# Eight PSUM banks dealt anew between chunk preparation and RWKV chains

## The chip, the cores and the metric

The kernel runs on one core of one Trainium2 chip. The time is the device time of one execution in microseconds. Five engines work side by side, each through its own queue in order: TensorE (PE; its weight loads stand as PEld), VectorE (DVE), ScalarE (ACT), GpSimd (POOL) and SyncE (SP), which here issues most of the DMAs. PE writes its results to PSUM alone, which has eight banks of 512 float32 per partition; DVE and ACT empty them.

## The reference

One layer over 512 latent tokens and 256 context tokens of width 2048. RMSNorm with modulation from a condition vector (w_mod), one projection that feeds two groups of heads, an output projection, a gated feed-forward network with a 3x3 depthwise convolution, and a final RMSNorm. The mLSTM group has four heads in two directions. The RWKV group has 16 heads of width 64, also in two directions, and its state goes from token to token:

```
def step(s, xs):                       # state s: 64 x 64 per head
    r_t, w_t, k_t, v_t, kk_t, a_t = xs
    s = (s * w_t[:, :, None, :]
         - jnp.einsum("bhvk,bhk->bhv", s, kk_t)[..., None] * (kk_t * a_t)[:, :, None, :]
         + v_t[..., :, None] * k_t[..., None, :])
    return s, jnp.einsum("bhvk,bhk->bhv", s, r_t)
```

The context is scanned first from a zero state; each direction of the latent tokens starts from that direction's last context state.

## The kernel before, in words

**RWKV in chunks.** The scan is cut into chunks of 64 tokens: four for the context, eight for x. Heads go in pairs, one head on partitions 0 to 63 and one on 64 to 127; there are eight pairs. For each pair four things happen, one after the other.

- The preparation (`pair_shared`, `prep`). For x it is called once per direction; for the context both directions go through at once. It makes the decays and gates (matmuls L701, tanh L704), the running sum (L437), the operands KR and BK, and then in two halves of four chunks: products of BK and KR (L747) into two PSUM tiles, four masks (L750) into the SBUF tile r_Gp, a store of r_Gp to DRAM (L751). After that, again in two halves: a scaled copy of BK (L756, into r_cum), four transposes (L759) into one PSUM tile, four copies (L763) into r_sg, a store (L764). r_sg, r_cum, r_Gp, r_KR and r_BK have one buffer each, and r_sg is also what the tanh of the next preparation writes.
- The solve (`tsolve`): it inverts the triangular blocks, on DVE (L798, L799) and with small matmuls (L816, L821) behind a transpose (L810).
- The chain (`chain`, `chain_step`): eight steps for x, four for the context. In a step the state M and the values V are multiplied with the chunk's operands, ACT copies the sum to r_Rs (L872), matmuls give U, ACT copies that to r_U (L880), matmuls give the change of M, which DVE adds (L892), and for x the output y (L899 for the first half of the chunks, L901 after).
- The bonus and the finalization of y (`bonus`, `finalize_pair`).

Two pairs form a job for solve and chain.

**PSUM.** The eight banks are dealt to three tags: "acc" (the projections, two), "pre" (preparation, the early mLSTM heads, the w_mod sums, finalization, two) and "R" (solve and chain, four). A chain step of one pair takes two banks, one per head, with both directions in each; so the steps of two pairs, which alternate in the program, go through four banks.

**Order.** The program is unrolled. A planner lays down each engine's order ahead of time: it goes through the instructions by priority (the order in the program, with weight loads and their splits moved ahead) and through an assumed timeline, and puts the first one that is ready there next on its engine. So projections are put between the steps of preparation and chain. On the chip each engine then follows that order and waits where an operand or buffer is late. In the program, x goes pair by pair: `x_pair(p + 1)` with projections for the next pair, `x_job(p)` with solve or chain for earlier pairs and the preparation of pair p, then w_mod sums (`ada_late`: DVE sums L232, with one buffer am for the loads). After the last pair come its solve and chain, the mLSTM projections (`x_head`), three early mLSTM heads, which use SBUF tiles of the preparation, and the output projection, whose first half needs the mLSTM heads 0 and 1 and the RWKV pairs 0 to 3. In the step as it was, this is what the change turns round:

```
for src in range(2):           # 0: the state M, 1: the values V
    for k, u in enumerate(us): # the two directions of one pair
        for j in kinds:        # two products for x, one for the context
            for h in range(2): # the two heads, a bank each
```

Of the kernel before, what the change touches and what calls it, by code (L numbers as in the profile page):

```python
# [11 lines left out]
ALU = mybir.AluOpType  # L12
# [3 lines left out]
P = 128  # L16
# [80 lines left out]
def body(tc, A, dbg=None):  # L97
    nc = tc.nc
    pe, dve, act, pool, sp = nc.tensor, nc.vector, nc.scalar, nc.gpsimd, nc.sync
# [3 lines left out]
    def nm(s):  # L103
        cnt[0] += 1
        return f"{s}_{cnt[0]}"
# [17 lines left out]
    wp = Pool("wp")  # L123
    hp = Pool("hp")
    sm = Pool("sm")
    PB = {"acc": 2, "pre": 2, "R": 4}

    def PS(tag, shape):
        return ps.tile(list(shape), F32, tag=tag, name=nm(tag), bufs=PB[tag])

    def DT(tag, shape, bufs=1):
        return dr.tile(list(shape), F32, tag=tag, name=nm(tag), bufs=bufs)
# [11 lines left out]
    rk = Pool("rk")  # L144
# [192 lines left out]
    def wload(src, shape, slot=None):  # L337


        n = max(shape[1] // WPARTS, 1)  # L340
        his, los = [], []
        wn[0] += 1
        with tc.high_priority(ahead_[0]), tc.issue_after(last_wm[0].ins) if W_TIE < wn[0] <= 3 else nullcontext():
            raw = wp("wraw", shape, WRAW)
            if not isinstance(src, list):
                src = [src]
            m = shape[1] // len(src)
            for i, a in enumerate(src):
                last_w[0] = sp.dma_start(raw[:, i * m:i * m + m], a)
            for i in range(0, shape[1], n):  # L350
                sh = [P, n] + list(shape[2:])
                if slot is None:
                    hi = wp("whi", sh, WBUF, F32R)
                    lo = wp("wlo", sh, WBUF, F32R)
                else:
                    hi, lo = slot[:, 0, i:i + n], slot[:, 1, i:i + n]
                split(raw[:, i:i + n], hi, lo)
                his.append(hi)
                los.append(lo)
        return (lambda i: his[i // n][:, i % n]), (lambda i: los[i // n][:, i % n])  # L360
# [288 lines left out]
    LOHI = (slice(0, 64), slice(64, 128))  # L649
# [176 lines left out]
    def chain_load(u, tt):  # L826

        cu = u.c0 + 2 * tt
        o = rk("r_GK", [P, 2, 512], 6)[:, :, 0:3 * u.kc + 128]
        sp.dma_start(o, u.S_d[:, cu:cu + 2, :])  # L830
        return o

    def chain_v(p, seg, nch):

        t = rk("r_V", [P, 8, 64], 3)[:, 0:nch]
        for h, hs in enumerate(LOHI):
            o = (p % 2) * 128 + 64 * h
            sp.dma_start(t[hs], v_d[seg][p // 2, :, :, o:o + 64].rearrange("a (b t) v -> t (a b) v", t=64))
        return t

    def chain_step(us, ops, cs, V, y, first, last):

        x = us[0].seg == "x"
        kc = us[0].kc
        bank = [PS("R", [P, 8, 64]) for _ in range(2)]
        pos = (0, 1) if cs[0] < cs[1] else (1, 0)
        opened = {}

        def mm(h, half, o, w, rhs):

            hs = LOHI[h]
            out = bank[h][LOHI[half], o, :]
            at = opened.get((h, half))
            f = dict(stop=True, skip_group_check=True)
            if at is None:
                opened[(h, half)] = pe.matmul(out, w[hs], rhs[hs], start=True, **f)
                return
            with tc.issue_after(at.ins):
                pe.matmul(out, w[hs], rhs[hs], start=False, **f)  # L859

        w = [o[:, c % 2] for o, c in zip(ops, cs)]
        kinds = range(2) if x else range(1)
        for src in range(2):
            for k, u in enumerate(us):
                for j in kinds:
                    for h in range(2):
                        o = 2 * kc * src + 64 * j
                        mm(h, h if j == 0 else 1 - h, pos[k], w[k][:, o:o + 64], u.M if src == 0 else V[:, cs[k], :])
        Rs = rk("r_Rs", [P, 2, 64], 3)
        U = rk("r_U", [P, 2, 64], 3)  # L870
        for h, hs in enumerate(LOHI):
            act.copy(Rs[hs], bank[h][hs, 0:2, :])  # L872
        for k, u in enumerate(us):
            for h in range(2):
                mm(h, 1 - h, 2 + pos[k], w[k][:, kc:kc + 64], Rs[:, pos[k], :])
            for h in range(2):
                if not last:
                    mm(h, h, 2 + pos[k], w[k][:, 3 * kc + 64:3 * kc + 128], V[:, cs[k], :])
        for h, hs in enumerate(LOHI):
            act.copy(U[hs], bank[h][LOHI[1 - h], 2:4, :])  # L880
        for k, u in enumerate(us):
            for h in range(2):
                if not last:
                    mm(h, h, 2 + pos[k], w[k][:, 3 * kc:3 * kc + 64], U[:, pos[k], :])
            for h in range(2):
                if x:
                    mm(h, 1 - h, pos[k], w[k][:, kc + 64:kc + 128], U[:, pos[k], :])
        if not last:
            for k, u in enumerate(us):
                g = u.g0 + cs[k]  # L890
                for h, hs in enumerate(LOHI):
                    dve.scalar_tensor_tensor(u.M[hs], u.M[hs], u.gC[hs, g:g + 1], bank[h][hs, 2 + pos[k], :], ALU.mult, ALU.add)  # L892
        if x:
            lo, hi = min(cs), max(cs)
            for h in range(2):
                hs = LOHI[1 - h]
                out = y[hs, lo:hi + 1:hi - lo, :]
                if first:
                    dve.tensor_copy(out, bank[h][hs, 0:2, :])  # L899
                else:  # L900
                    dve.tensor_tensor(out, bank[h][hs, 0:2, :], out, ALU.add)  # L901

    def chain(pairs, mid):

        x = pairs[0][0].seg == "x"
        nch = pairs[0][0].nch
        Vs, ys = [], []
        for us in pairs:
            Vs.append(chain_v(us[0].p, us[0].seg, nch))
            ys.append(rk("r_yt", [P, 8, 64], 2) if x else None)  # L910
            for u in us:
                if not x:
                    Mst[(u.p, u.d)] = rk("r_M", [P, 64], 16)
                    pool.memset(Mst[(u.p, u.d)], 0.0)
                u.M = Mst[(u.p, u.d)]
        n = nch // 2
        for i in range(n):
            if x and i == 1:
                mid()
            ops = [[chain_load(u, i if u.d == 0 else n - 1 - i) for u in us] for us in pairs]  # L920
            for c in range(2 * i, 2 * i + 2):
                for us, o, V, y in zip(pairs, ops, Vs, ys):
                    chain_step(us, o, (c, nch - 1 - c), V, y, c < nch // 2, x and c == nch - 1)
        if x:
            for us, y in zip(pairs, ys):
                y_d = us[0].y_d = DT("yr_d", [4, P, 128], 8)
                for h in range(2):
                    sp.dma_start(y_d[:, :, 64 * h:64 * h + 64].rearrange("a (b t) v -> t (a b) v", t=64), y[LOHI[1 - h]])
            mid()
# [153 lines left out]
    for q, (k0, k1) in enumerate(KPARTS):  # L1083
        ks = slice(k0, k1)
        n = (k1 - k0) * P
# [47 lines left out]
    def do_chain(n=1):  # L1133
        if len(chain_q) >= n:
            job = [t for _ in range(n) for t in chain_q.pop(0)]
            chain([us for _, us, _ in job], fin_step)
            fin_q.extend(t for t in job if t[2] is not None)
# [215 lines left out]
    last, end = [], iter(())  # L1353
    for g in range(NG):
# [7 lines left out]
        for cs in (slice(0, NX),) if g < NG - 1 else (slice(0, NX // 2), slice(NX // 2, NX)):  # L1362
            n = cs.stop - cs.start
            su = ev() if g == NG - 1 else None
            for m2 in range(0, KT, 2):
                if g < NG - 1:
                    hi, lo = wload(A["wdn"][g, m2 // 2], [P, 2, GF, P])
                elif cs.start == 0:
                    last.append(wload(A["wdn"][g, m2 // 2], [P, 2, GF, P], hp("H", [P, 2, 2, GF, P], 8, F32R)))
                if g == NG - 1:  # L1370
                    hi, lo = last[m2 // 2]
# [129 lines left out]
```

## Time and profile before

| | |
|---|---|
| median of three runs | 3376.81 us (3371.88 to 3381.96) |
| the profiled execution | 3379.97 us |
| its span | 3378.2 us |
| mean granted PE clock | 0.945 of full speed |
| busy | PE 3108.0 us (92%), DVE 2165.9 (64%), ACT 1192.4 (35%), POOL 59.6 (2%) |
| DMA | 548.53 MB, 162 GB/s in the mean |

The profile is one execution. A busy PE is one with a matmul under way; it says nothing of how dense they are. The page's slices of 84 us show where PE has holes and where its granted clock falls: both lie between 1400 and 1700 us.

```
PE   8998899999989898657599899999999999999998
PEclk9999998899989898767799999999999999999999
```

In the rows below, times are microseconds from the start of the span, unless a column says ns.

### The profile page before, as it was taken

To read this page: it belongs to the slowest core of one execution; us is meant where nothing else is said; L and a number is where in the kernel's file an instruction comes from. 1 tells how busy PE (TensorE), PEld (TensorE's weight loads), DVE (VectorE), ACT (ScalarE), POOL (GpSimd) and SP (SyncE) were. 2 spreads that over 40 slices of the span, in tenths; PEclk is the share of its full clock that TensorE was granted. 3 is DMA by queue.
4 is the path that set the end of the run, shared out by engine and by line. 5 is a ranking of instruction groups with operands and counts; after the bars stand their busy time and mean duration, and the time that the engine had idled before them with its cause. 6 is when DMAs were issued, how large, how long until landed. Compare 5 with 4: busy or idle time off the path is not lost.

```text
span 3378.2 us, 54574 instructions
## 1 busy us (share of the span) xinstructions
PE 3108.0 (92%) x21030; PEld 2509.7 (74%) x21030; DVE 2165.9 (64%) x4178; ACT 1192.4 (35%) x2414; POOL 59.6 (2%) x113
## 2 busy tenths in 40 slices
PE   8998899999989898657599899999999999999998
PEld 5687777777768687545477688888888888888887
DVE  2587776688688778645644788455555555555657
ACT  4355554344444344222223432222222222322323
POOL 0000100010000000000000000000000000000000
PEclk9999998899989898767799999999999999999999
DMA  8877555557767687565844255222223222222232
GB/s 284 305 243 220 155 159 163 166 174 234 208 208 239 215 247 240 181 197 178 257 153 157 77 199 194 94 94 98 95 95 99 94 96 98 94 98 96 94 100 100
DMA packets 394387, 548.53 MB, mean 162 GB/s; under 512 B 151664, under 2 KB 272776, under 8 KB 393872
## 3 DMA queue, kind: packets, MB, share of 16 engines
q1 hardware_dynamic: 384480, 531.67, 49.3%
q10 hardware_dynamic: 9648, 13.37, 1.1%
q8 instruction: 166, 2.72, 0.3%
q14 instruction: 93, 0.76, 0.1%
HBM read 457.49 MB, written 87.47 MB: 161 GB/s over the span
## 4 chain that ended last, share of the span: by engine, by line
PE 53%; DMA 9%; DVE 6%; ACT 1%; issue 1%; SPq 1%; DVEq 0%; ACTq 0%
PE acc L371 10%; PE acc L372 10%; PE acc L370 10%; PE acc L1376 5%; PE acc L1378 5%; PE acc L1377 5%; DMA am<-in_wmod 3%; PE acc L1262 1%; PE pre L621 1%; PE acc L1263 1%; PE acc L1264 1%; DVE adacc L232 1%; DMA Sx_d<-r_sg 1%; PE R L859 1%; DMA x_d<-ev 1%
## 5 line engine op out<-in xcount | busy, mean ns | idle before, releaser
L299 ACT CAST whi<-wraw 128x512 fp32r<-128x512 f32 (+1 forms) x948 | 569.6, 604 | 1307.7 <-PE acc L371 678.6
L300 DVE TENSOR_TENSOR wlo<-wraw,whi 128x512 fp32r<-128x512 f32 (+1 forms) x948 | 628.4, 666 | 429.0 <-ACT whi L299 423.1
L370 PE MATMUL acc<-H,whi 128*128 128x512 f32 x1920 | 761.2, 396 | 6.1 <-ACT ev L520 4.0
L372 PE MATMUL acc<-H,wlo 128*128 128x512 f32 x1920 | 762.3, 397 | 1.2 <-DVE wlo L300 1.2
L371 PE MATMUL acc<-H,whi 128*128 128x512 f32 x1920 | 760.4, 396 | 0.0
L370 PEld LDWEIGHTS acc<-H,whi 128*128 128x128 f32 x1920 | 363.8, 189 | 87.5 <-ACT ev L520 4.3
L372 PEld LDWEIGHTS acc<-H,wlo 128*128 128x128 f32 x1920 | 364.2, 190 | 82.0 <-issue 4.9
L371 PEld LDWEIGHTS acc<-H,whi 128*128 128x128 f32 x1920 | 364.4, 190 | 78.8 <-issue 2.9
L1380 DVE SCALAR_TENSOR_TENSOR x<-acc,mod,x 128x512 f32<-128x512 f32 (+1 forms) x192 | 135.6, 706 | 221.7 <-PE acc L1378 221.6
L1324 DVE SCALAR_TENSOR_TENSOR f_cv<-upad,fvec,f_cv 128x512 f32<-128x512 f32 x352 | 263.8, 749 | 7.2
L1376 PE MATMUL acc<-fh,whi 128*128 128x512 f32 x640 | 253.2, 396 | 0.0
L1377 PE MATMUL acc<-fl,whi 128*128 128x512 f32 x640 | 253.1, 396 | 0.0
L1378 PE MATMUL acc<-fh,wlo 128*128 128x512 f32 x640 | 253.1, 396 | 0.0
L232 DVE SCALAR_TENSOR_TENSOR adacc<-am,csil,adacc 128x512 f32<-128x512 f32 x240 | 179.4, 748 | 83.7 <-DMA am<-in_wmod 81.6
L403 PE MATMUL acc<-whi,H 128*128 128x256 f32 x512 | 159.8, 313 | 2.2 <-ACT r_E L720 1.5
L405 PE MATMUL acc<-wlo,H 128*128 128x256 f32 x512 | 158.6, 311 | 1.6 <-DVE wlo L300 1.6
L404 PE MATMUL acc<-whi,H 128*128 128x256 f32 x512 | 156.0, 305 | 0.0
L1378 PEld LDWEIGHTS acc<-fh,wlo 128*128 128x128 f32 x640 | 120.2, 188 | 29.1
L1377 PEld LDWEIGHTS acc<-fl,whi 128*128 128x128 f32 x640 | 120.2, 188 | 29.0
L1376 PEld LDWEIGHTS acc<-fh,whi 128*128 128x128 f32 x640 | 120.2, 188 | 29.0
L1262 PE MATMUL acc<-H,whi 128*128 128x512 f32 x256 | 104.6, 414 | 32.4 <-DVE ev L1271 18.6
L750 DVE TENSOR_TENSOR r_Gp<-pre,c_gmask 64x512 f32<-64x512 f32 (+1 forms) x192 | 115.1, 599 | 18.1 <-DMA Sx_d<-r_Gp 11.6
(346 smaller groups left out, 4751.6 us busy)
## 6 DMA issues: line engine op xcount, KB each, us to landing
am<-in_wmod SPq DMA_DIRECT2D x128, 512.0 KB
wraw<-in_wup SPq DMA_DIRECT2D x88, 512.0 KB
wraw<-in_wgate SPq DMA_DIRECT2D x88, 512.0 KB
wraw<-in_wdn SPq DMA_DIRECT2D x88, 512.0 KB
wraw<-in_wcm SPq DMA_DIRECT2D x72, 512.0 KB
r_GK<-Sx_d SPq DMA_DIRECT2D x64, 512.0 KB
wraw<-in_wtm SPq DMA_DIRECT2D x56, 512.0 KB
Sx_d<-r_Gp SPq DMA_DIRECT2D x32, 512.0 KB
```

Of the source, the lines that this page charges most:

```text
L232: dve.scalar_tensor_tensor(acc, wm[:, k % 2], csil[:, k:k + 1], acc, ALU.mult, ALU.add)
L299: act.copy(hi, t)
L300: dve.tensor_tensor(lo, t, hi.bitcast(F32), ALU.subtract)
L370: pe.matmul(pt[:, :n], hi(k8), H.h(k), start=k == 0, stop=False)
L371: pe.matmul(pt[:, :n], hi(k8), H.l(k), start=False, stop=False)
L372: pe.matmul(pt[:, :n], lo(k8), H.h(k), start=False, stop=k == KT - 1)
L403: pe.matmul(o, H.h(k)[:, xs], hi(k4), start=first, stop=False, skip_group_check=True)
L405: pe.matmul(o, H.h(k)[:, xs], lo(k4), start=False, stop=k == KT - 1, skip_group_check=True)
L1324: dve.scalar_tensor_tensor(cv, u[:, a:a + GH, b:b + GW], fvec[:, f, tap:tap + 1], cv, ALU.mult, ALU.add)
L1376: pe.matmul(pt, hi(m)[:, k, :], th[:, cs], start=k == 0, stop=False)
L1377: pe.matmul(pt, hi(m)[:, k, :], tl[:, cs], start=False, stop=False)
L1378: pe.matmul(pt, lo(m)[:, k, :], th[:, cs], start=False, stop=k == GF - 1)
```

## The change

"pre" gets four banks and "R" two. A chain step now takes both pairs of a job and both directions, four units, in one pair of banks: one bank for each head, and in it four column blocks of 64 for the sums and four for the changes. So a copy to r_Rs or r_U moves 256 columns in place of 128, and there are half as many; r_Rs and r_U are one buffer of twice the width in place of three. Products with V are put before those with M. The updates of M and y keep their shapes and number.

```
-    PB = {"acc": 2, "pre": 2, "R": 4}
+    PB = {"acc": 2, "pre": 4, "R": 2}
...
-    def chain_step(us, ops, cs, V, y, first, last):
+    def chain_step(units, first, last):
...
-        for src in range(2):
-            for k, u in enumerate(us):
-                for j in kinds:
+        for src in (1, 0):
+            for u, w, c, V, n in units:
+                for j in range(2 if x else 1):
                     for h in range(2):
                         o = 2 * kc * src + 64 * j
-                        mm(h, h if j == 0 else 1 - h, pos[k], w[k][:, o:o + 64], u.M if src == 0 else V[:, cs[k], :])
-        Rs = rk("r_Rs", [P, 2, 64], 3)
-        U = rk("r_U", [P, 2, 64], 3)
+                        mm(h, h if j == 0 else 1 - h, n, w[:, o:o + 64], V[:, c, :] if src else u.M)
+        Rs = rk("r_Rs", [P, 4, 64], 1)
+        U = rk("r_U", [P, 4, 64], 1)
         for h, hs in enumerate(LOHI):
-            act.copy(Rs[hs], bank[h][hs, 0:2, :])
+            act.copy(Rs[hs], bank[h][hs, 0:4, :])
...
         for h, hs in enumerate(LOHI):
-            act.copy(U[hs], bank[h][LOHI[1 - h], 2:4, :])
+            act.copy(U[hs], bank[h][LOHI[1 - h], 4:8, :])
...
             for c in range(2 * i, 2 * i + 2):
-                for us, o, V, y in zip(pairs, ops, Vs, ys):
-                    chain_step(us, o, (c, nch - 1 - c), V, y, c < nch // 2, x and c == nch - 1)
+                units = []
+                for k, (us, os_, V, y) in enumerate(zip(pairs, ops, Vs, ys)):
+                    us[0].y = y
+                    for j, (u, o) in enumerate(zip(us, os_)):
+                        cu = nch - 1 - c if j else c
+                        units.append((u, o[:, cu % 2], cu, V, 2 * k + (j if 2 * c < nch - 1 else 1 - j)))
+                chain_step(units, c < nch // 2, x and c == nch - 1)
```

## Rows read from the trace of the kernel before

**Rows 1.** Busy time by stretch: engines, instructions, granted clock, DMA share, GB/s.

```profile
570.00:1366.00 796.00, 731.03 (x7976) 592.65 (x7974) 614.76 (x1371) 331.34 (x763) 25.18 (x40) 0.93 0.68 211
1395.00:1660.00 265.00, 152.27 (x1590) 111.88 (x1589) 145.50 (x355) 66.37 (x196) 1.72 (x8) 0.68 0.64 200
1960.00:3378.00 1418.00, 1401.67 (x6320) 1157.38 (x6319) 841.88 (x1292) 401.60 (x668) 0.00 (x0) 1.00 0.32 107
```

**Rows 2.** PE's waits, whole span: waiter, what ended it, sum, times, longest.

```profile
PE R L816 <- DVE t_X L810: 26.8, 6, 11.2
PE pre L238 <- DVE adacc L232: 22.9, 1, 22.9
PE acc L1262 <- DVE ev L1271: 18.6, 1, 18.6
...
PE R L859 <- ACT r_U L880: 12.1, 11, 1.7
...
PE R L859 <- ACT r_Rs L872: 9.3, 8, 3.0
...
PE R L856 <- DVE r_yt L899: 6.3, 10, 1.6
```

**Rows 3.** Timeline (start, duration, instruction): first and last of the x preparations.

```profile
570.21 1.12 PE L701 MATMUL pre<-r_lw,r_up 128*128 128x512 f32 x2
...
1364.76 1.50 ACT L763 COPY r_sg<-pre 64x256 f32<-64x256 f32 x4 [0.19 <-ACT r_Rs L872]
```

**Rows 4.** Timeline of DVE: the masks of two preparations.

```profile
1029.95 2.81 DVE L750 TENSOR_TENSOR r_Gp<-pre,c_gmask 64x512 f32<-64x512 f32 x4
...
1037.84 2.81 DVE L750 TENSOR_TENSOR r_Gp<-pre,c_gmask 64x512 f32<-64x512 f32 x4
...
1186.13 2.81 DVE L750 TENSOR_TENSOR r_Gp<-pre,c_gmask 64x512 f32<-64x512 f32 x4
...
1196.85 2.81 DVE L750 TENSOR_TENSOR r_Gp<-pre,c_gmask 64x512 f32<-64x512 f32 x4
```

**Rows 5.** Timeline of SP's queue: stores of the first of these preparations.

```profile
1032.79 0.37 SPq L751 DMA_DIRECT2D Sx_d<-r_Gp  x1
...
1043.16 0.58 SPq L764 DMA_DIRECT2D Sx_d<-r_sg  x1
...
1053.32 1.57 SPq L764 DMA_DIRECT2D Sx_d<-r_sg  x1
```

**Rows 6.** Timeline of PE: the same preparation.

```profile
1034.51 1.49 PE L747 MATMUL pre<-r_KR,r_BK 64*128 64x128 f32 x16
...
1040.78 0.60 PE L759 MATMUL pre<-c_ident,r_cum 128*128 128x128 f32 x4
```

**Rows 7.** Timeline of ACT: the same preparation and the next one's tanh.

```profile
1041.41 1.50 ACT L763 COPY r_sg<-pre 64x256 f32<-64x256 f32 x4 [0.68 <-PE pre L759]
...
1049.46 1.50 ACT L763 COPY r_sg<-pre 64x256 f32<-64x256 f32 x4 [6.55 <-PE acc L404]
...
1059.83 0.67 ACT L704 ACTIVATE r_sg<-pre,c_vecs 128x512 f32<-128x512 f32 x1
```

**Rows 8.** Groups by line: busy us, mean ns, idle before and its releasers.

```profile
L892 DVE SCALAR_TENSOR_TENSOR r_M<-r_M,r_gC,R 64x64 f32<-64x64 f32 x352 | 87.5, 278 | 28.5 <-PE R L859 21.9 <-ACT r_U L880 2.7
...
L880 ACT COPY r_U<-R 64x128 f32<-64x128 f32 x192 | 49.8, 260 | 80.7 <-PE R L859 75.1 <-DVE t_X L799 1.6 <-ACT ev L520 0.4
...
L899 DVE COPY r_yt<-R 64x128 f32<-64x128 f32 x64 | 18.5, 289 | 1.0
```

**Rows 9.** Timeline: the third x chain's last bank, the next solve.

```profile
1372.75 0.28 DVE L901 TENSOR_TENSOR r_yt<-R,r_yt 64x128 f32<-64x128 f32 x1
...
1447.87 1.92 PE L816 MATMUL R<-t_X,t_Y 32*32 32x32 f32 x64 [9.65 <-DVE t_X L810]
```

**Rows 10.** DVE's waits from 200 to 1960 us.

```profile
DVE adacc L232 <- DMA am<-in_wmod: 74.5, 44, 5.2
```

More of the change, by code (lines that the diff above doesn't have):

```diff
@@ L839, in chain_v @@
         return t
-    def chain_step(us, ops, cs, V, y, first, last):
-        x = us[0].seg == "x"
-        kc = us[0].kc
+    def chain_step(units, first, last):
+        x = units[0][0].seg == "x"
+        kc = units[0][0].kc
         bank = [PS("R", [P, 8, 64]) for _ in range(2)]
-        pos = (0, 1) if cs[0] < cs[1] else (1, 0)
         opened = {}
@@ L859, in mm @@
                 pe.matmul(out, w[hs], rhs[hs], start=False, **f)
-        w = [o[:, c % 2] for o, c in zip(ops, cs)]
-        kinds = range(2) if x else range(1)
-        for src in range(2):
-            for k, u in enumerate(us):
-                for j in kinds:
+        for src in (1, 0):
+            for u, w, c, V, n in units:
+                for j in range(2 if x else 1):
                     for h in range(2):
                         o = 2 * kc * src + 64 * j
-                        mm(h, h if j == 0 else 1 - h, pos[k], w[k][:, o:o + 64], u.M if src == 0 else V[:, cs[k], :])
@@ L869, in chain_step @@
-        Rs = rk("r_Rs", [P, 2, 64], 3)
-        U = rk("r_U", [P, 2, 64], 3)
+                        mm(h, h if j == 0 else 1 - h, n, w[:, o:o + 64], V[:, c, :] if src else u.M)
+        Rs = rk("r_Rs", [P, 4, 64], 1)
+        U = rk("r_U", [P, 4, 64], 1)
         for h, hs in enumerate(LOHI):
-            act.copy(Rs[hs], bank[h][hs, 0:2, :])
-        for k, u in enumerate(us):
+            act.copy(Rs[hs], bank[h][hs, 0:4, :])
+        for u, w, c, V, n in units:
             for h in range(2):
-                mm(h, 1 - h, 2 + pos[k], w[k][:, kc:kc + 64], Rs[:, pos[k], :])
+                mm(h, 1 - h, 4 + n, w[:, kc:kc + 64], Rs[:, n, :])
@@ L876, in chain_step @@
             for h in range(2):
                 if not last:
-                    mm(h, h, 2 + pos[k], w[k][:, 3 * kc + 64:3 * kc + 128], V[:, cs[k], :])
+                    mm(h, h, 4 + n, w[:, 3 * kc + 64:3 * kc + 128], V[:, c, :])
         for h, hs in enumerate(LOHI):
-            act.copy(U[hs], bank[h][LOHI[1 - h], 2:4, :])
-        for k, u in enumerate(us):
+            act.copy(U[hs], bank[h][LOHI[1 - h], 4:8, :])
+        for u, w, c, V, n in units:
             for h in range(2):
                 if not last:
-                    mm(h, h, 2 + pos[k], w[k][:, 3 * kc:3 * kc + 64], U[:, pos[k], :])
+                    mm(h, h, 4 + n, w[:, 3 * kc:3 * kc + 64], U[:, n, :])
@@ L885, in chain_step @@
             for h in range(2):
                 if x:
-                    mm(h, 1 - h, pos[k], w[k][:, kc + 64:kc + 128], U[:, pos[k], :])
+                    mm(h, 1 - h, n, w[:, kc + 64:kc + 128], U[:, n, :])
         if not last:
-            for k, u in enumerate(us):
-                g = u.g0 + cs[k]
+            for u, w, c, V, n in units:
+                g = u.g0 + c
                 for h, hs in enumerate(LOHI):
-                    dve.scalar_tensor_tensor(u.M[hs], u.M[hs], u.gC[hs, g:g + 1], bank[h][hs, 2 + pos[k], :], ALU.mult, ALU.add)
+                    dve.scalar_tensor_tensor(u.M[hs], u.M[hs], u.gC[hs, g:g + 1], bank[h][hs, 4 + n, :], ALU.mult, ALU.add)
@@ L893, in chain_step @@
         if x:
[L894 to L901, printed above, removed]
+            for k in range(0, len(units), 2):
+                cs = [units[k][2], units[k + 1][2]]
+                lo, hi = min(cs), max(cs)
+                y = units[k][0].y
+                for h in range(2):
+                    hs = LOHI[1 - h]
+                    out = y[hs, lo:hi + 1:hi - lo, :]
+                    if first:
+                        dve.tensor_copy(out, bank[h][hs, k:k + 2, :])
+                    else:
+                        dve.tensor_tensor(out, bank[h][hs, k:k + 2, :], out, ALU.add)
```

## The prediction

> **What bounds the kernel now.** I read the table of busy time by stretch first. From 1960 us on PE (TensorE) is busy 1401.67 of 1418 us at full clock, and the change touches nothing there [rows 1]. Two earlier stretches matter [rows 1]: from 570 to 1366 us PE is busy 731.03 of 796 us with DVE at 614.76, and from 1395 to 1660 us PE is busy only 152.27 of 265 us, at a granted clock of 0.68, a mix of the 1.2 and 2.4 GHz levels. So some 113 us of PE stand empty in the second, and 65 in the first.
>
> Next, PE's waits [rows 2]: the largest belong to the tail (the solve's matmuls behind the transpose L810, 26.8 us; one wait of 22.9 us for a w_mod sum; 18.6 us at the start of the output projection). The waits inside the chain steps, for r_U, for r_Rs and for the y copy L899, sum to 12.1 + 9.3 + 6.3 = 27.7 us.
>
> Why does the tail begin where it does? The timeline shows it. The sixteen preparations of x chunks (eight pairs, two directions) run strictly one after the other, because their SBUF buffers r_sg, r_cum, r_Gp, r_KR and r_BK are single. The first starts with its matmul L701 at 570.21, the last ends with its copy L763 at 1364.76 + 1.50 [rows 3]: 796 / 16 = 49.7 us each. Projections fill PE beside them, and by about 1395 none is left, so solve, first mLSTM head and second mLSTM head run with PE nearly empty. The bound up to 1660 us is therefore a chain of latencies with PE work beside it; a preparation that takes less time moves the tail forward under projections that still have to run.
>
> **The preparation, part one of the change.** I followed one preparation, from the masks on. The first half's four masks L750 start at 1029.95 and end at 1032.76; the second half's start at 1037.84 and end at 1040.65, 7.9 us later; in another preparation (1186.13 and 1196.85) the distance is 10.7 us, mean 9.3 [rows 4]. The distance isn't PSUM: r_Gp is one buffer, whose store L751 is issued at 1032.79 [rows 5], and the second masks wait for it to land. PE shows what PSUM does [rows 6]: the second half's L747 starts at 1034.51, after the first half's masks have emptied both banks, and the transposes L759 of the first half only at 1040.78, right behind the second masks, because with two "pre" banks they need one that the second half holds. Behind them hangs what the next preparation waits for: the copies L763 into r_sg at 1041.41 and, after the first store of r_sg, at 1049.46 [rows 7]; the second store is issued at 1053.32 [rows 5], and the next preparation's tanh L704 writes r_sg at 1059.83 [rows 7].
>
> With four "pre" banks the two halves take four different ones, the transposes take those that the first masks emptied, and they don't wait for the second masks. Upper bound of the gain: the whole 9.3 us per preparation, 149 us over sixteen. Lower bound: nothing, if DVE or the stores bind. DVE's work per preparation is 614.76 / 16 = 38.4 us [rows 1], 77% of 49.7 and 95% of 40.4, so the upper bound would want a DVE without a gap in a queue that runs in order. I take a little under half, 4 us: DVE would stand at 38.4 / 45.7 = 84%, and the second masks keep their 2.81 us in that queue. 16 x 4 = 64 us. What is late next is the store of r_sg, then DVE.
>
> Does that reach the end? From 570 to 1660 us PE works 731 + 29 (the stretch between the two, counted as full) + 152 = 912 us in 1090. At the first stretch's share, 731 / 796 = 92%, it would take 993: up to 97 us can be given back before PE itself binds. So the 64 us pass in full, with no credit for the clock, and of the upper bound only 97.
>
> The eight context preparations before 570 us have the same order, but x pairs also need their projections, which fill PE there; I count nothing; were that cover gone, 8 x 4 = 32 us more would come back, within the 97. The early mLSTM heads draw on "pre" too: nothing to 10 us, taken as nothing, because their waits in the tail are on DVE and on loads.
>
> **The chains, part two.** Instructions per step of two pairs: the 32 or fewer matmuls of each stage stay; V's come before M's. ACT copies go from eight to four. A copy of 128 columns takes 260 ns (192 of r_U [rows 8], and as many of r_Rs); a PSUM copy of 256 columns takes 1.50 / 4 = 375 ns [rows 7]. So 384 x 260 = 100 us become 192 x 375 = 72 us of ACT. 28 us less on an engine that isn't the bound: nothing. DVE's 352 updates of M (278 ns) and 64 + 64 of y (289 ns) stay as they are [rows 8].
>
> What is added is a wait. Before, each pair had its own two banks, so that one pair's matmuls ran while the other's were emptied. After, the two banks are shut from the first copy to the last y addition: per x step 2 x 2 x 0.375 (copies) + 8 x 0.278 (M) + 4 x 0.289 (y) = 1.5 + 2.2 + 1.2 = 4.9 us, a little less in context steps. Queued behind on PE is whatever the planner placed next, mostly projections that need no R bank. There are 16 context and 32 x steps; the last eight lie in the tail, so 40 steps lie beside projections. Bounds: a gain of 27.7 us (all chain waits on PE go, since PE changes over half as often) and a loss of 40 x 4.9 = 196 us (every one uncovered). I take nothing: the rows nearest to it are the present waits for exactly such copies, 27.7 us over all steps, so projections cover most of this latency now. A longer chain alone costs nothing: the third x chain reads its last bank at 1372.75, and the next solve, the first to want an R bank, starts its matmuls at 1447.87 [rows 9], 75 us later. The solves lose their second pair of banks: 0 to 5 us at the last solve, taken as 0, since that wait is for L810's data [rows 2].
>
> The Trainium skill, page "Perfetto Trace Analysis", section "Optimizing Tensor Performance", part "Matmuls", says that independent groups of matmuls should go round different PSUM banks, so that one is emptied while the next computes; it speaks for the preparation and against the chains. By it for the chains alone the second rival's time would come out; the trace bears it out only as far as the 27.7 us of chain waits show.
>
> **Sum.** The profiled execution took 3379.97 us: its span of 3378.2 us and 1.8 us around it. 3380 - 64 = 3316. The median of the three runs is 3376.81, 3 us below the profiled one, so the forecast is 3313 us.
>
> **Rivals.** First: something else holds the preparation. The store of r_Gp and the DVE queue stand right behind the PSUM wait; if the transposes move forward but the second copy still waits for its place in the ACT or SP queue, half a microsecond each is left, 8 us: 3369. For it: the second r_sg store is issued 2.4 us after its copies end [rows 5, 7]. Against it: DVE has 23% free.
>
> Second, on the other side: the chains stall PE. Each step shuts both banks for 4.9 us, and PE, in order, stops if the planner put a chain matmul too early. If half goes uncovered, 40 x 2.45 = 98 us, less the 64: 3377 + 34 = 3411. It decides from 64 / 40 = 1.6 us of stall per step on. Against it: the 27.7 us now; for it: nothing else of the chain is left to run in that time.
>
> Third: the tail eats half the gain. The w_mod sums go through one buffer, and DVE waits for it 74.5 us in 44 waits, 1.7 us each and 5.2 at most [rows 10]; these loads are paced by their own transfers. If preparations end 64 us sooner, about one more chunk of eight loads falls into the tail: 8 waits of up to 5.2 us, 42 us: 3377 - 22 = 3355.
>
> **How the numbers follow.** About 0.3%, 10 us, is what a measurement of this kernel can tell from no change. Forecast 0.56 (its own range 3265 to 3355), first rival 0.16, second 0.17, third 0.11. Faster: nearly all of the first and third and a little of the first rival, 0.66. Same: most of the first rival, 0.15. Slower: the second and a rest, 0.19. The low end is the PE limit and the heads' bound, 3377 - 97 - 10, with 8 us for the clock in a filled tail: 3262. The high end, 3395, leaves out the worse half of the second rival.
>
> **What the changed profile would show.** Right: L759 starts within 2 us of the end of the first masks; the sixteenth preparation ends near 1300 us instead of 1366; the tail holds projections and a clock above 0.8; 96 copies of r_Rs at some 370 ns. Wrong: L759 still follows the second masks, or follows the first and L704 doesn't come earlier (first rival); PE's waits for r_Rs, r_U and y above 60 us (second); the stretch from the last preparation to the output projection longer than before, with L232 waiting (third).

## The result: slower by 0.8%

The changed kernel takes 3403.22 us (median of four runs, 3397.96 to 3406.01) against 3374.35 us for the kernel before, also a median of four runs: 1.0081 times as long, 95% interval 1.0058 to 1.0104. The forecast was 3313 us. The profiled execution took 3401.15 us with a span of 3399.3 us, 21 us more than before.

The table of busy time by stretch (columns as in [rows 1]), of the kernel after:

```profile
1050.00:1100.00 50.00, 50.00 (x629) 41.92 (x628) 20.49 (x49) 15.47 (x29) 0.00 (x0) 1.00 0.46 140
1300.00:1700.00 400.00, 240.39 (x2938) 189.62 (x2936) 242.80 (x590) 117.84 (x269) 2.73 (x13) 0.65 0.66 207
...
1960.00:3378.00 1418.00, 1415.64 (x6359) 1168.24 (x6358) 842.91 (x1280) 404.92 (x671) 0.00 (x0) 1.00 0.33 107
```

The same view of the kernel before, for the first two of these stretches:

```profile
1050.00:1100.00 50.00, 48.65 (x565) 41.24 (x565) 38.23 (x65) 25.37 (x47) 0.30 (x2) 0.97 0.85 253
1300.00:1700.00 400.00, 269.26 (x2700) 202.57 (x2699) 242.34 (x579) 108.99 (x306) 2.12 (x11) 0.74 0.64 202
```

The last stretch, from 1960 us on, is as full as in [rows 1]. What was lost lies ahead of it. From 1300 to 1700 us PE stands empty for 400 - 240.39 = 160 us, before for 131; that the 29 us between them are near to the time lost (21 us between the two profiled spans, 29 between the medians) doesn't make them its cause, as the experiments show. And there is a strange stretch before that: from 1050 to 1100 us PE is busy without a gap, but DVE only 20.49 us of 50, where before it was busy for 38.23.

The timeline of the kernel after (start, duration, engine, line, instruction) shows the preparation at work, the place where DVE runs empty, and the chains:

```profile
535.00 1.02 PE L701 MATMUL pre<-r_lw,r_up 128*128 128x512 f32 x2
...
884.04 0.63 ACT L667 ACTIVATE r_t<-r_kk 128x512 f32<-128x512 f32 x1
...
958.91 0.76 ACT L870 COPY r_Rs<-R 64x256 f32<-64x256 f32 x2 [2.35 <-DVE t_X L799]
...
1111.57 0.60 PE L977 MATMUL pre<-c_ident,r_y 128*128 128x128 f32 x4
1112.01 1.02 PE L669 MATMUL pre<-r_t,c_bones 128*128 128x512 f32 x2
...
1115.61 0.67 ACT L704 ACTIVATE r_sg<-pre,c_vecs 128x512 f32<-128x512 f32 x1
...
1134.20 2.82 DVE L750 TENSOR_TENSOR r_Gp<-pre,c_gmask 64x512 f32<-64x512 f32 x4
...
1135.73 0.63 PE L759 MATMUL pre<-c_ident,r_cum 128*128 128x128 f32 x4 [1.07 <-DVE r_Gp L750]
...
1141.32 2.81 DVE L750 TENSOR_TENSOR r_Gp<-pre,c_gmask 64x512 f32<-64x512 f32 x4 [1.17 <-DMA Sx_d<-r_Gp]
1142.14 1.50 ACT L763 COPY r_sg<-pre 64x256 f32<-64x256 f32 x4
...
1237.53 0.63 ACT L667 ACTIVATE r_t<-r_kk 128x512 f32<-128x512 f32 x1
...
1320.27 1.11 PE L977 MATMUL pre<-c_ident,r_y 128*128 128x128 f32 x4
1321.17 1.92 PE L669 MATMUL pre<-r_t,c_bones 128*128 128x512 f32 x2
...
1380.70 1.50 ACT L763 COPY r_sg<-pre 64x256 f32<-64x256 f32 x4 [4.58 <-PE pre L759]
...
1448.26 3.27 PE L816 MATMUL R<-t_X,t_Y 32*32 32x32 f32 x61
1448.43 0.48 DVE L902 TENSOR_TENSOR r_yt<-R,r_yt 64x128 f32<-64x128 f32 x2 [0.52 <-PE R L859]
...
1652.81 0.76 ACT L870 COPY r_Rs<-R 64x256 f32<-64x256 f32 x2 [1.16 <-PE R L859]
...
1663.06 0.48 DVE L902 TENSOR_TENSOR r_yt<-R,r_yt 64x128 f32<-64x128 f32 x2
...
1679.60 1.11 PE L977 MATMUL pre<-c_ident,r_y 128*128 128x128 f32 x4 [22.22 <-DVE r_y L971]
1695.60 1.12 PE L977 MATMUL pre<-c_ident,r_y 128*128 128x128 f32 x4 [14.90 <-DVE r_y L971]
1696.51 7.97 PE L605 MATMUL pre<-r_kr,r_KR 128*128 128x512 f32 x12
...
1816.10 0.79 PE L1268 MATMUL acc<-H,whi 128*128 128x512 f32 x1 [8.88 <-ACT H L299]
```

The end of the same way in the kernel before, where the finalization's transposes are L971 and the output projection is L1262:

```profile
1589.73 0.28 DVE L901 TENSOR_TENSOR r_yt<-R,r_yt 64x128 f32<-64x128 f32 x1 [1.97 <-PE R L859]
...
1675.25 0.63 PE L971 MATMUL pre<-c_ident,r_y 128*128 128x128 f32 x4 [0.58 <-DVE r_y L965]
1675.72 1.02 PE L605 MATMUL pre<-r_kr,r_KR 128*128 128x512 f32 x2
...
1797.08 0.79 PE L1262 MATMUL acc<-H,whi 128*128 128x512 f32 x1 [6.94 <-ACT H L299]
```

- The transposes L759 of the first half start at 1135.73, before the end of the first masks (1134.20 + 2.82), and long before the second masks (1141.32). Before they stood right behind the second masks [rows 4, 6]. From tanh L704 (1115.61) to the end of the last copy L763 (1143.64) this preparation takes 28.0 us; the one in [rows 7] took 41.8, from its tanh at 1009.14 to 1049.46 + 1.50. That is one preparation each; means stand below.
- Yet the sixteenth preparation ends at 1382.2, 16 us later than before [rows 3], though the first began 35 us sooner. One pair stands still for 228 us: the input of its sum of squares L669 is written at 884.04, and the matmul runs at 1112.01, right behind four transposes L977. Those belong to the finalization of the first pair, whose chain starts at 958.91. The same happens again at 1237.53 and 1321.17: 84 us.
- The third x chain's last addition to y, at 1448.43, and the next solve, at 1448.26, now touch each other. Between them lay 75 us [rows 9]. But the solve starts when it did before (1447.87): up to here this path has lost nothing and gained nothing.
- The loss lies behind it. The fourth chain's last addition to y ends 73 us later than before, and the last finalization's transposes start 20 us later (1695.60 against 1675.25), now behind waits of PE of 22.22 and 14.90 us. Right behind them, in both kernels, come the first matmuls L605 of the last two mLSTM heads, which take "pre" banks (1696.51 against 1675.72). The second half of the output projection needs these heads; it starts at 1816.10 against 1797.08, 19 us later, and the span is 21 us longer.

PE's waits in the chain steps, of the kernel after (columns as in [rows 2]):

```profile
PE R L856 <- DVE r_yt L902: 20.1, 7, 6.3
PE R L859 <- ACT r_U L878: 17.4, 7, 6.2
...
PE R L859 <- ACT r_Rs L870: 12.2, 7, 3.0
PE R L856 <- DVE r_yt L900: 12.2, 8, 3.2
```

They sum to 61.9 us. The 27.7 us of [rows 2] are without the second kind of work on y (L902 here, L901 before), for which PE waited in the kernel before:

```profile
PE R L856 <- DVE r_yt L901: 3.0, 5, 1.5
```

So the same four waits were 30.7 us there.

### The profile page after: what moved, and what is told of

Same layout as the page of the kernel before. It is cut to its first block, busy times and chain, and to the rows that moved or that the text cites. A ratio compares the mean times of both kernels' runs of the same rounds, so it can differ in the third digit from the quotient of the medians.

```text
span 3399.3 us, 54225 instructions
## 1 busy us (share of the span) xinstructions
PE 3083.4 (91%) x21030; PEld 2509.1 (74%) x21030; DVE 2170.8 (64%) x4178; ACT 1181.5 (35%) x2235; POOL 45.7 (1%) x113
## 4 chain that ended last, share of the span: by engine, by line
PE 57%; DVE 10%; DMA 9%; issue 2%; ACT 2%; SPq 1%; DVEq 0%; ACTq 0%
PE acc L372 10%; PE acc L370 10%; PE acc L371 10%; PE acc L1382 5%; PE acc L1384 4%; PE acc L1383 4%; DMA am<-in_wmod 3%; PE acc L1268 1%; PE acc L1269 1%; PE acc L1270 1%; DVE adacc L232 1%; DVE r_Gp L750 1%; PE R L859 1%; PE pre L621 1%; DVE r_M L890 1%
## 5 line engine op out<-in xcount | busy, mean ns | idle before, releaser
L404 PE MATMUL acc<-whi,H 128*128 128x256 f32 x512 | 151.8, 297 | 0.0
L405 PE MATMUL acc<-wlo,H 128*128 128x256 f32 x512 | 148.9, 293 | 3.1 <-DVE wlo L300 3.1
L403 PE MATMUL acc<-whi,H 128*128 128x256 f32 x512 | 150.5, 294 | 0.5 <-DVE ev L434 0.5
```

Of the source, the lines that this page charges most:

```text
L403: pe.matmul(o, H.h(k)[:, xs], hi(k4), start=first, stop=False, skip_group_check=True)
L404: pe.matmul(o, H.l(k)[:, xs], hi(k4), start=False, stop=False, skip_group_check=True)
```

## The experiments

**The theory after this reading.** A tag's banks are dealt in the order of the program. Finalization stands in the program inside an earlier job and takes a "pre" bank; preparation of a later pair gets the bank after it, and so waits for the whole chain that the finalization needs (the tie). Whether it is the planner's order on PE or a bank that holds it, the rows don't tell: PE has other work meanwhile. **Rivals:** the two R banks make the chains slow, and all the rest follows; or the merged steps as such do.

**e1: the new deal with the old steps.** Kernel before, with one line:

```
-    PB = {"acc": 2, "pre": 2, "R": 4}
+    PB = {"acc": 2, "pre": 4, "R": 2}
```

> The banks of the change (four pre, two R), the chain steps of before, one pair at a time. Theory (tie): each preparation of an odd pair waits for the finalization of an earlier pair, because both take their banks from pre in program order, and that finalization waits for a whole chain; so what counts is how long the stream of solves and chains on R is. With two R banks and one pair per step the two pairs of a job no longer overlap at all: an x chain takes longer than the 111 to 154 us of after, the waits before the preparations of pairs 5 and 7 grow, 3420 to 3500 us. Rival (PE stalls in the merged steps): no merged step is left, so it is no slower than before, 3300 to 3380 us.

Measured: 3500.86 us, ratio 1.0383 [1.0364, 1.0403], at the upper end of the theory's range. The tie is in its timeline (L971 is finalization's transpose there):

```profile
867.00 0.63 ACT L667 ACTIVATE r_t<-r_kk 128x512 f32<-128x512 f32 x1
...
1225.39 1.11 PE L971 MATMUL pre<-c_ident,r_y 128*128 128x128 f32 x4 [3.84 <-DVE r_y L965]
1226.30 1.91 PE L669 MATMUL pre<-r_t,c_bones 128*128 128x512 f32 x2
```

A pair waits 359 us for its preparation, and the last one ends at 1473.5, 91 us later than in the changed kernel. So with two banks for the chains the merged steps are what keeps the loss small.

**e2: the merged steps with the old deal.** Kernel after, with the `PB` of before (2, 2, 4).

> The merged chain steps, the banks of before (two pre, four R). Theory (tie): two chain steps may overlap and solves have their own banks again, so chains start and end as in before or sooner; preparations are as slow as before (transposes behind the second masks): 3350 to 3390 us. Rival (PE stalls in merged steps): the merged step is there, so the loss is there as well, 3395 us or more.

Measured: 3391.14 us, 1.0053 [1.0034, 1.0072], between the theory's range and the rival's. In its trace (of a run of 3402.86 us) preparation is as slow as before, and the same pair's sum of squares waits from 1015.4 to 1088.5, 73 us. So the merged steps alone cost about 18 us in this program. The deal on top of them costs 12 more by the medians, but the two intervals overlap: that part isn't shown.

**e3: a bank for finalization alone.**

```
-    PB = {"acc": 2, "pre": 4, "R": 2}
+    PB = {"acc": 2, "pre": 3, "R": 2, "fin": 1}
...
-        pt = PS("pre", [P, 512])
+        pt = PS("fin", [P, 512])
```

> The change with one edit: the transposes of the finalization get a bank of their own, taken from pre (three pre, two R, one for them). Program order is the same. Theory (tie through the PSUM tag): the wait of 228 us between the sum of squares of pair 5 and its matmul (884 to 1112 us) falls below 40 us, and that of pair 7 as well; preparations end before 1300 us (after: 1380), and the time falls to 3320 to 3370 us. Rival (PE stalls): same waits inside the steps, 3385 to 3410 us. Rival (the SP queue or program order holds the preparation, not PSUM): waits and time as in after, 3390 to 3410 us.

Measured: 3342.21 us, 0.9911 [0.9892, 0.9930]: faster than both, as the theory had it. The merged steps and the two R banks are still there, so neither rival explains it. No sum of squares waits over 47 us, and the preparations end at 1183.5.

**e4: the finalizations later in the program.** A job's odd chains no longer call `fin_step`; it is called twice behind the preparation of an odd pair.

```
-            do_chain(2)
+            do_chain(2, lambda: None)
...
+        if p % 2 and p > 3:
+            fin_step()
+            fin_step()
```

> The change with one edit: the finalization steps that stood inside the second and third x chain come in the program after the preparation of that pair; banks as in the change. Theory (tie): as with a bank of its own, the waits before pairs 5 and 7 go, 3320 to 3370 us. Rival (PE stalls in the steps): 3385 to 3410 us. If this is fast and a bank of its own is not, the tie is program order in another resource than PSUM.

Measured: 3390.08 us, 1.0053 [1.0033, 1.0072]: not the 3320 to 3370 of the theory, but in the rival's range. The trace says why, and it isn't the rival's reason. The tie moved with the program: now it is the next pair that waits, 156 us, again right behind finalization's transposes:

```profile
963.48 0.63 ACT L667 ACTIVATE r_t<-r_kk 128x512 f32<-128x512 f32 x1 [0.27 <-DVE r_BK L733]
...
1118.55 0.60 PE L977 MATMUL pre<-c_ident,r_y 128*128 128x128 f32 x4
1119.80 1.10 PE L669 MATMUL pre<-r_t,c_bones 128*128 128x512 f32 x2
```

**e5: finalization on the chains' tag.** One word of the kernel after: the transposes take a bank of "R", on which they stand behind the chain anyway.

```
-        pt = PS("pre", [P, 512])
+        pt = PS("R", [P, 512])
```

> The change with one word different: the finalization's transposes take an R bank, not a pre bank (four pre, two R). Theory (tie through the order in which pre banks are dealt): as with a bank of their own, no preparation waits more than 50 us for its sum of squares; preparations end near 1180 us; 3330 to 3350 us. If instead the third pre bank was what helped in the run with a bank of their own, or chance, the time stays above 3370 us.

Measured: 3356.50 us, 0.9949 [0.9932, 0.9967], 47 us less than the changed kernel, and 6 us above the range expected. Its timeline:

```profile
887.09 0.64 ACT L667 ACTIVATE r_t<-r_kk 128x512 f32<-128x512 f32 x1
...
906.72 2.05 PE L669 MATMUL pre<-r_t,c_bones 128*128 128x512 f32 x2
...
966.30 0.36 ACT L870 COPY r_Rs<-R 64x256 f32<-64x256 f32 x1
...
1134.79 1.51 ACT L763 COPY r_sg<-pre 64x256 f32<-64x256 f32 x4 [9.41 <-DMA Sx_d<-r_sg]
...
1407.36 0.70 DVE L810 STREAM_TRANSPOSE t_X<-t_Y 128x512 f32<-128x512 f32 x1
...
1446.00 0.48 DVE L902 TENSOR_TENSOR r_yt<-R,r_yt 64x128 f32<-64x128 f32 x2 [0.53 <-PE R L859]
1446.87 3.27 PE L816 MATMUL R<-t_X,t_Y 32*32 32x32 f32 x61
...
1572.44 3.76 PE L605 MATMUL pre<-r_kr,r_KR 128*128 128x512 f32 x4
...
1630.73 0.76 ACT L870 COPY r_Rs<-R 64x256 f32<-64x256 f32 x2 [1.61 <-PE R L859]
...
1776.32 0.80 PE L1268 MATMUL acc<-H,whi 128*128 128x512 f32 x1 [10.60 <-ACT H L299]
```

The wait of 228 us is one of 20, and the sixteenth preparation ends at 1136.3, 230 us sooner than before [rows 3]. Of these 230 us the end gets 18. So the preparations don't set it. The last solve is ready for its matmuls at 1408.06, but they start at 1446.87, right behind the third chain's last addition to y: with two R banks the solve stands behind the chain. The time gained comes from behind the solve: the third mLSTM head starts at 1572.44 in place of 1696.51, ahead of the last finalization (1716.7), and the second half of the output projection at 1776.32 in place of 1816.10.

Every trace here shows the same place. From the start of that second half to the end of the span it is 1580 to 1584 us in all fourteen. In the five whose finalization takes a "pre" bank (before, after, e1, e2, e4) the third head's L605 starts within 1 us of the last finalization's transposes, and 117 to 124 us later the second half starts; in the nine others the third head starts 41 to 145 us ahead of them.

**e6: the same word in the kernel before.**

> The kernel before (two pre, four R, one pair per step) with the same word different. Theory: before, the tie cost 29 and 48 us before pairs 5 and 7 at most, and the transposes of the preparation still stand behind the second masks, so its preparations still take some 45 us each: 3355 to 3372 us. If the tie is the whole story and the second pair of pre banks is worth nothing, this one is as fast as the change with that word, 3330 to 3350 us.

Measured: 3375.23 us, 1.0007 [0.9991, 1.0022]. That is above the 3355 to 3372 of the theory: in the kernel before the tie cost nothing. The wait in question was 29.5 us (1026.20 to 1055.68), and without the tie it is 26.4.

**e7 and e8: what makes a merged step long.** e7 is e5 with the chain steps ahead in the planner's order; e8 is e5 with the products with M put first again.

```
+        with tc.high_priority(1000):
+            chain_step(units, c < nch // 2, x and c == nch - 1)
```

```
-        for src in (1, 0):
+        for src in (0, 1):
```

> The change with the finalization on R and the chain steps moved 1000 places ahead in the planner's priority. If the stream of solves and chains sets the end once the tie is gone, because each step waits behind projections and preparation on PE and DVE, an x chain step falls from some 18 to 21 us to 12 to 15 and the time by 10 to 40 us against the run before it, 3295 to 3330 us. If the stream isn't the bound, or its waits aren't for its place in the queues, within 10 us of that run.

> The change with the finalization on R and, in the merged step, the products with the state before those with V, as in the kernel before. If V first shortens the step because its products run while the state is being updated, this one is slower by some 32 steps x 0.5 to 1 us, 5 to 30 us; if the banks are shut until the last y addition anyway, the two are within 5 us.

Measured: 3354.59 us, 0.9942 [0.9926, 0.9959], and 3356.88 us, 0.9951 [0.9932, 0.9970]. Neither differs from e5.

**e9: the merged steps, untied, with the old deal.** e5 with `PB` 2, 2, 4.

> The changed kernel's merged steps, finalization's transposes on the tag R, and the banks as before: two for preparation, four for the chains. Theory (two shut banks make a chain step of the untied kernel long: there the steps took some 20 us, and the end hangs on the chains): with a second pair of banks the first matmuls of a step need not wait for the last y addition of the step before; steps of 15 to 17 us, 8 steps in each of four x chains, the preparations back at some 45 us each because the transposes L759 stand behind the second masks again; the output projection starts near 1515 and the time is 3335 to 3350 us. Rival (the bank isn't what makes the step long; the two engines' queues are): steps stay at 18 to 21 us, the slower preparations come on top, 3375 to 3395 us, as the merged steps alone took with finalization untouched (3391).

Measured: 3336.61 us, 0.9900 [0.9882, 0.9919]: 54 us less than e2 by that one word, and 20 less than e5 by the deal alone (measured at different times; the kernel before took between 3370 and 3376 us beside them, and the intervals don't touch). Its timeline and, below it, its stretch from 1300 to 1700 us:

```profile
1326.88 1.50 ACT L763 COPY r_sg<-pre 64x256 f32<-64x256 f32 x4 [5.62 <-DMA Sx_d<-r_sg]
...
1568.58 0.37 ACT L870 COPY r_Rs<-R 64x256 f32<-64x256 f32 x1
```

```profile
1300.00:1700.00 400.00, 307.39 (x2926) 237.86 (x2927) 252.16 (x626) 110.76 (x289) 1.86 (x9) 0.79 0.67 210
```

Its preparations end 192 us later than e5's (1328.4 against 1136.3), its chains 62 us sooner (1569 against 1631), and it is the faster of the two. PE stands empty for 93 us from 1300 to 1700. With four R banks the last solve's matmuls start 8 us behind its transpose on DVE (1393.3 and 1401.2); with e5's two it is 39.5 us.

**e10 and e11: banks in between.** e10 is e5 with `PB` 2, 3, 3; e11 is e3 with 2 for "pre", 3 for "R", 1 for "fin".

> The changed kernel with finalization's transposes on the tag R, three banks for preparation and three for the chains. Theory (the shut banks make the step long): with a third bank half of each step's first matmuls can start before the y additions of the step before; steps of 17 to 19 us instead of 20, preparations nearly as short as with four banks (29 to 37 us), 3335 to 3350 us against the 3356 of two chain banks. Rival (queues make the step long): 3354 to 3365 us, steps at 20 us.

> The changed kernel with a bank of its own for finalization's transposes, two banks for preparation and three for the chains (the version with three and two took 3342 us). Theory (both count: preparation wants more than two banks, chains more than two): the preparation loses what the third bank gave, some 5 us each, the chain steps gain 1 to 3 us each; 3340 to 3370 us. Rival (the chains' banks alone set the end once finalization is untied): below 3335 us. Second rival (only the preparation's banks count): 3370 us or more, like the merged steps alone.

Measured: 3352.16 us, 0.9943 [0.9922, 0.9964], and 3344.39 us, 0.9926 [0.9901, 0.9951]. In e10 the x steps take 18.9, 20.0, 15.8 and 19.1 us in the four chains, hardly less than e5's; the time lies between the theory's range and the rival's, and decides nothing. In e11 they take 19.0, 18.4, 15.5 and 14.9, and the time is in the theory's range.

**e12: the tie moved to a third tag.** e9 with finalization on the projections' tag, a word again.

```
-        pt = PS("R", [P, 512])
+        pt = PS("acc", [P, 512])
```

> The changed kernel's merged steps, two banks for preparation and four for the chains, as in the version of 3337 us, but finalization's transposes take an acc bank, of which the projections have two, instead of one of the tag R. Theory (a tag is dealt in the order of the program, so whoever shares it with a finalization waits for the chain behind it): the tie now falls on whichever projections stand behind a finalization in the program; PE loses its filling work for as long as a chain takes, there are single waits of 50 us and more between two matmuls of the projections, and the time is above the 3337 us, 3350 to 3450. Rival (the tie was special to the preparation, and R is the scarce tag): the chain stream is relieved of the transposes, 3320 to 3337 us.

Measured: 3498.62 us, 1.0365 [1.0342, 1.0388], 162 us more than e9 and more than the theory gave. Its timeline, in which no matmul of PE writes an acc bank between the first two lines, and the stretch around it:

```profile
811.02 0.40 PE L372 MATMUL acc<-H,wlo 128*128 128x512 f32 x1
...
1027.57 1.11 PE L977 MATMUL acc<-c_ident,r_y 128*128 128x128 f32 x4
...
1352.75 1.11 PE L977 MATMUL acc<-c_ident,r_y 128*128 128x128 f32 x4
1353.52 0.78 PE L370 MATMUL acc<-H,whi 128*128 128x512 f32 x1
```

```profile
900.00:1300.00 400.00, 281.04 (x3682) 225.09 (x3678) 293.73 (x691) 123.15 (x258) 10.64 (x21) 0.60 0.64 191
```

All projections stand still for 216 us until the first finalization has come through, and after a short burst once more until 1352.75. The tie is a property of the tag's order; whoever stands behind finalization on its tag waits for it.

**The runs side by side**, by deal (pre, R) and by whether finalization shares a tag with the preparation:

| steps, deal | tied | untied (on R) |
|---|---|---|
| single pairs, 2 and 4 | 1 (before) | 1.0007 (e6) |
| single pairs, 4 and 2 | 1.0383 (e1) | not run |
| merged, 2 and 4 | 1.0053 (e2) | 0.9900 (e9) |
| merged, 4 and 2 | 1.0081 (after) | 0.9949 (e5) |

## Why the prediction was wrong

**The preparation: the mechanism was right, the gain larger than forecast.** The transposes left the second masks as described, and the merged copies took 365 ns (r_Rs) and 367 (r_U) where 375 were put down. In e5, where no finalization holds them, sixteen preparations take 1136.3 - 534.8 = 601.5 us, 37.6 each; in e9, which differs by the deal alone, 47.2; before, 49.7. So the deal gives some 10 us each instead of the 4 that were taken: about the upper bound of 9.3, which was taken to want a DVE without a gap. The context preparations, counted as nothing, gave their share too: the first x preparation starts 35 us sooner (535.00 against 570.21), where 32 were priced as a possibility.

**"So the 64 us pass in full" failed.** It was put down as -64 us. With merged steps the deal costs 12 us by the medians (e2 to after, 3391 to 3403; the intervals overlap), and untied 20 (e9 to e5), though the preparations end 192 us sooner there. The argument took the end of the sixteenth preparation for what starts the tail. With two R banks it isn't: solves and chains go through them one after the other, from 966 to 1631 us in e5. From its transpose on DVE to its first matmul a solve waits there 80, 96 and 39.5 us, each time for the end of a chain; with four banks (e9) 23, 1 and 8. So the last solve starts at 1446.87 in e5 and at 1448.26 in the changed kernel, as before (1447.87). Some of e5's loss to e9 may be that its finalizations share those two R banks: e3, with two R banks and finalization off them, takes 3342.

**"A longer chain alone costs nothing" failed too.** It read its slack of 75 us in one place, behind the third x chain [rows 9], and asked only who wants the next R bank. Two things use up that slack. The steps got longer: the first copy of r_Rs of a step follows that of the step before after 14.4 to 15.9 us in the four chains before, after 17.8, 21.6, 14.6 and 21.5 us in the kernel after. And the chain's end has a second customer that was not looked for: finalization, and through the order of the "pre" banks the preparation of a later pair. That wait was already there, 29.5 us long, and free (e6); with a chain that starts later and takes longer it became 73 us in e2 and 228 in the kernel after, in which PE ran on projections, chain and solve without a preparation (50.00 of 50 us, DVE at 20.49). That the tail lacks these projections, and that this costs time, isn't shown: from 1300 to 1700 us PE stands empty for 113 us in e5 and for 59 in e10, whose times lie 4 us apart. The runs show the size of the tie: 47 us in the changed kernel (e5) and 54 with the merged steps alone (e9).

**"The early mLSTM heads ... taken as nothing" failed where the time was lost.** The reason given was that their waits in the tail are on DVE and on loads. But the last two heads take their "pre" banks behind the last finalization, and that one waits for the fourth chain. Before, some 85 us lay between the chain's last addition to y and these transposes; after, 32. So of the 73 us by which the chain ends later, 20 reach the heads, 19 the output projection and 21 the end. In e2's trace it is 23 us at the transposes and 23 at the end. Moving the finalization off "pre" frees the preparation and the heads at once; no run here frees the heads alone.

**The sum.** Forecast was -64 + 0. Measured: +18 for the steps (e2) and, by the medians, +12 for the deal, about the 29 us between 3374.35 and 3403.22.

**The rivals.** The first (3369) fell: preparation did get faster. The third (3355) isn't seen: from the last preparation to the first matmul of the output projection it is 166.5 us (1382.2 to 1548.7), before 176.5. The second comes out nearest in time, 3411, and its sign, waits in the steps above 60 us, is there with 61.9. But it priced 98 us of such waits on PE, and they grew by 31; its mechanism is a part at best, since with the same steps and the tie gone e9 is 1.0% faster than before. No rival named the tie.

**What stays open.** Why a merged step takes 17 to 21 us where projections stand beside it, and 10.1 in e5's third chain, where few do. Neither the planner's priority (e7) nor the order of V and M (e8) moves it; a second pair of banks takes 1 to 5 us off it in three of four chains (e9: 19.2, 16.8, 17.3, 16.1 against 20.1, 20.2, 10.1, 21.0), a third bank next to nothing. Why the merged steps gain 1.0% when untied, though each takes longer than the single steps did, is shown in part: e9's preparations end at 1328.4, 38 us sooner than before, and its last solve starts 47 us sooner. Why they end sooner is open; that the steps copy with half the instructions (35.0 us for r_Rs where it was 49.8) is one candidate, not tested. Open too is what holds the last two heads in the untied kernels. e9 and e3, which both beat the two kernels, can't be told apart (0.9900 [0.9882, 0.9919] and 0.9911 [0.9892, 0.9930]).

## What to carry to other kernels

Before banks are dealt anew, list for each tag everything that takes one, in the order of the program, and ask of each what it waits for: a stage that shares a tag with a late stage inherits its wait, and one word (which tag the late stage takes) was worth 47 to 162 us in the merged kernels, and nothing in the kernel before (e6). When an early stage gets faster, check the stage that is serial behind it before counting the gain: 230 us at the preparations' end were 18 at the kernel's. And follow a loss back from the end: a wait of 228 us looked like the cause, but the last solve still started on time; the loss shows where the last finalization stands ahead of the last two heads.

## What the runs showed of the hardware

Where PE had less work beside its waits, its granted clock was mostly lower. With a short burst of projections alone (e12, 900 to 1300 us) PE was busy 281 of 400 us at a mean of 0.60, a mix of its levels of 1.2 and 2.4 GHz; e9 had 353 busy us there at 0.92. From 1300 to 1700 us the clock was 0.65 after, 0.74 before and 0.79 in e9. It isn't the order of the times for all: e5 had 0.73 and e3 0.74 there, and both are faster than the kernel before. How much of a time the clock makes wasn't measured.
